# Two token tiles in one product at the small levels of a gated linear attention, in a one-core decoder block

## The chip, the cores and the metric

The kernel runs on one core of one Trainium2 chip. The metric is the device time of one execution in microseconds (us). The kernel before took 900.85 us in the median of three runs (900.52 to 900.86). One execution was recorded by the hardware profiler; it took 900.46 us, of which the profile shows a span of 898.7 us, from the first to the last recorded instruction.

## What is computed

The reference is one layer of a decoder with 512 tokens and width 1024, all in float32: a LayerNorm of the input, a combined input projection, a gated linear attention (GLA) with 4 heads beside a latent attention (MLA) with 8 heads, a gated merge and an output projection, then a squared-ReLU MLP of hidden width 4096, each sub-layer followed by a LayerNorm. The change touches the GLA scores only. Cut to them:

```python
def gla_chunked(q, k, v, log_a):          # per head: 512 tokens, dk 128, dv 256
    # S_t = diag(a_t) S_{t-1} + k_t^T v_t,  o_t = q_t S_t
    b = cumsum(log_a)
    scores[i, j] = sum_d q[i, d] * k[j, d] * exp(b[i, d] - b[j, d])    # j <= i
    o = scores @ v
```

The reference does it in chunks of 64 with a carried state; the kernel computes the scores of all 512 tokens directly.

## The kernel before, in words

**Names.** P is 128 (the partitions), T is 512 (the tokens), NT is 4 (token tiles of 128), GH is 4 heads. Tokens are on the free axis of `qk[:, 0]` (keys) and `qk[:, 1]` (queries), with the 128 channels of a head on the partitions.

**The levels.** The decay of a score is exp(b_i - b_j), a number per channel, so that it has to be put into the two operands of a product without overflow. `gla_levels(h)` (L606) does this by halving. At level s = 1, 2, 4 up to 256 the 512 tokens are cut into blocks of 2s tokens; a score belongs to level s if its key is in the left half of a block and its query in the right half. For these the decay splits into two factors, both at most one, from the running sums in `rp`: one from the key to the border of the halves, one from the border to the query. `vec(s)` makes, for each level, E = exp(rp/16) on ScalarE (L624), then M = E times the left keys and the right queries on VectorE (L626), and `advance(s)` carries the sums in `rp` on to the next level with two additions on GpSimd (L619, L620). So E, the two additions and the next E follow one another.

**The products.** For levels 2 to 64, L680 makes one product per token tile: the stationary operand is the tile's 128 columns of M (keys and queries together; at levels 32 and 64 only the first 96 or 64), the moving operand its 64 right queries. Only the rows of left keys, and of these only those whose block is the query's, hold wanted scores. A float32 product is issued as two passes on TensorE, each with its own load of the stationary operand, so that a level and head have 8 passes. Levels 128 (L684) and 256 (L688) have two products each. Level 1 is made together with the diagonal by L663.

**The selection.** `take(s, p)` copies the wanted scores out of PSUM into `SD` (128 keys by 4 tiles by 128 queries, float32) with a predicated copy on VectorE (L636), under a mask `lmask` per level. The mask comes from DRAM as int32 (`lmi`) and is cast to uint8 once (L415). At a head's end SD is split into a high part (ScalarE, L697) and a remainder (GpSimd, L698) in `sd`, which `gla_out(h)` (L703) uses as stationary operands against the values.

**The order of the work.** The large products (`gemm_fm`, L221; `gemm_tm`, L246) run over steps k of two 128-row slices of weights each. After each step they call `tick`, which advances the side lanes (Python generators) by one `yield`: `lane_levels` goes through the levels of heads 0 to 3, and `lane_out` through the outputs. While `proj_v(0)`, `proj_r(0)`, `proj_v(1)`, `proj_r(1)` and the gate products run, the lanes fill in. `proj_v(1)` has a guard that steps `lane_levels` until head 1 is done, before its results are taken out of PSUM (L904, L912). The instructions of each engine are put into a fixed order by a planner that simulates the program at build time with a cost model, with the order of issue as the priority; on the chip every engine then follows its list, and TensorE waits at a product whose operand isn't there. `tc.issue_after(x)` holds what is issued on x's engine behind x.

**Buffers.** Products of the lanes go into 4 PSUM banks with the tag px; the large ones into 4 others (mm). SBUF tiles come from the pools A (24 slots), B (22 slots) and small ones. Weights come through `pump` (L157): a DMA on the SP queue, then a high part on ScalarE (L180) and a remainder on VectorE (L181), one entry ahead of the product that uses it.

The lines of the level products are these:

```python
for tt in range(NT):
    c = slice(tt * P, (tt + 1) * P)
    mm(p[:rows(s), tt * 64:(tt + 1) * 64].rearrange("p (n s) -> p n s", s=s),
       M[:, tt * P:tt * P + rows(s)], pairs(M[:, c], s)[:, :, 1, :], start=True, stop=True)
```

Of the kernel before, what the change touches and what calls it, by code (L numbers as in the profile page):

```python
# [19 lines left out]
P = 128  # L20
# [32 lines left out]
def tile_hybrid_block(ctx: ExitStack, tc: tile.TileContext, I, out, dbg=None):  # L53
# [22 lines left out]
    def B(shape, dt=F32, n="b"):  # L76
        return pb.tile(shape, dt, tag="B", name=nm(n))
# [10 lines left out]
    def f(ap):  # L88
        return ap.bitcast(F32)
# [256 lines left out]
    def ln_rows(src, dst, mv, on_act=False):  # L346
        bst = S([P, 2, 6], F32, "bst")
        for j in range(2):
            nc.vector.bn_stats(bst[:, j, :], src[:, j * T:(j + 1) * T])
        nc.vector.bn_aggr(mv, bst)  # L350
        vts(mv[:, 1:2], mv[:, 1:2], LN_EPS, None, op0=ALU.add)  # L351
        gtt(mv[:, 1:2], mv[:, 1:2], mhalf[:, 0:1], op=ALU.pow)  # L352
        if on_act:
            nmr = S([P, 1], F32, "nmr")
            stt(nmr, mv[:, 0:1], -1.0, mv[:, 1:2], op0=ALU.mult, op1=ALU.mult)
            act(dst, src, AF.Identity, scale=mv[:, 1:2], bias=nmr)
        else:
            vts(dst, src, mv[:, 0:1], mv[:, 1:2], op0=ALU.subtract, op1=ALU.mult)
# [38 lines left out]
    qag, kvg, glg, bga, bgt, ln1g, ln1b, neg, invf = [cb[:, cut[i]:cut[i + 1]] for i in range(9)]  # L397
    posi = consts.tile([P, NT], I32, name="posi")
    nc.scalar.dma_start(posi, I["positions"].rearrange("(t p) -> p t", p=P))
    lmask = consts.tile([P, len(LEVELS), 64], U8, name="lmask")  # L400
    lmi = B([P, len(LEVELS), 64], I32, "lmi")
    nc.scalar.dma_start(lmi, I["c_lmask"])
    wa2 = B([80, T], F32, "wa2")
    nc.gpsimd.memset(wa2, 0.0)
    for i in range(3):
# [3 lines left out]
    sn2 = consts.tile([P, NT, ROPE], F32, name="sn2")  # L409

    def prep():
        with tc.issue_after(last_in.ins):
            vts(hbg, bgt, 0.5, None, op0=ALU.mult)
            nc.vector.tensor_copy(negb, neg)
            nc.vector.tensor_copy(lmask, lmi)  # L415
        posf = consts.tile([P, NT], F32, name="posf")
        with tc.issue_after(last_in.ins):
            nc.vector.tensor_copy(posf, posi)
        ang = B([P, NT, 32], F32, "ang")
        for tt in range(NT):  # L420
            vts(ang[:, tt, :], invf, posf[:, tt:tt + 1], None, op0=ALU.mult)
        yield
        angs = []
        for sh in (0.0, 0.25):
            kq = B([P, NT, 32], F32, "kq")
            vts(kq, ang, 1.0 / (2.0 * math.pi), sh, op0=ALU.mult, op1=ALU.add)
            vts(kq, kq, MAGIC, None, op0=ALU.add)
            vts(kq, kq, MAGIC, None, op0=ALU.subtract)
            r = B([P, NT, 32], F32, "rr")
            stt(r, kq, -TWO_PI_1, ang, op0=ALU.mult, op1=ALU.add)  # L430
            stt(r, kq, -TWO_PI_2, r, op0=ALU.mult, op1=ALU.add)
            stt(r, kq, -TWO_PI_3, r, op0=ALU.mult, op1=ALU.add)
            vts(r, r, sh * 2.0 * math.pi, PI_F, op0=ALU.add, op1=ALU.min)
            vts(r, r, -PI_F, None, op0=ALU.max)
            angs.append(r)
            yield
        act(sn2[:, :, 32:], angs[0], AF.Sin)
        act(cs2[:, :, :32], angs[1], AF.Sin)
        nc.vector.tensor_copy(cs2[:, :, 32:], cs2[:, :, :32])
        vts(sn2[:, :, :32], sn2[:, :, 32:], -1.0, None, op0=ALU.mult)  # L440
        yield
# [158 lines left out]

    SS = [None] * GH

    def rows(s):
        return P - s if s >= 32 else P

    def gla_levels(h):  # L606
        qk = QK[h]
        QK[h] = None
        rp = A([P, 2, T], F32, "rp")
        nc.vector.tensor_copy(rp[:, 1, :], GL[h])  # L610
        nc.gpsimd.memset(rp[:, 0, :], 0.0)
        SD = B([P, NT, P], F32, "SD")
        SDf = SD.rearrange("p t i -> p (t i)")
        s128 = s256 = None

        def advance(s):
            Rv, Pv = pairs(rp[:, 0, :], s), pairs(rp[:, 1, :], s)
            n = T // (2 * s)
            gtt(Rv[:, :, 0, :], Rv[:, :, 0, :], Pv[:, :, 1, s - 1:s].to_broadcast([P, n, s]), op=ALU.add)  # L619
            gtt(Pv[:, :, 1, :], Pv[:, :, 1, :], Pv[:, :, 0, s - 1:s].to_broadcast([P, n, s]), op=ALU.add)  # L620

        def vec(s):
            E = B([P, T], F32, "E")
            act(pairs(E, s), lr(rp, s), AF.Exp, scale=1.0 / 16.0)  # L624
            M = B([P, T], F32, "M")
            vtt(pairs(M, s), pairs(E, s), lr(qk, s), op=ALU.mult)  # L626
            if s < 256:
                advance(s)
            return M

        def take(s, p):
            nonlocal s128, s256
            if s <= 64:
                n, m = 64 // s, rows(s)
                mk = lmask[:m, LEVELS.index(s), :].rearrange("p (n s) -> p n s", s=s)
                nc.vector.copy_predicated(  # L636
                    SDf[:m].rearrange("p (t n two s) -> p t n two s", t=NT, two=2, s=s)[:, :, :, 1, :],
                    mk[:, None].to_broadcast([m, NT, n, s]),
                    p[:m, :256].rearrange("p (t n s) -> p t n s", t=NT, s=s))
            elif s == 128:  # L640
                s128 = B([P, 2, 2, P], F32R, "s128")
                split(p[:, :256].rearrange("p (a b) -> p a b", b=P), s128[:, 0], s128[:, 1])
            else:
                s256 = A([P, 2, 2, 2 * P], F32R, "s256")
                split(p.rearrange("p (a b) -> p a b", b=256), s256[:, 0], s256[:, 1])


        q1 = B([P, NT, 64], F32, "q1")
        act(q1, pairs(rp[:, 1, :], 1)[:, :, 1, :], AF.Exp, scale=1.0 / 16.0)  # L649
        xs = [B([P, 2, 192], F32, "x1") for _ in range(2)]  # L650
        for i in range(2):
            t2 = slice(2 * i * P, 2 * (i + 1) * P)
            act(xs[i][:, :, :P], qk[:, 1, t2].rearrange("p (t i) -> p t i", i=P), AF.Copy)
            vtt(xs[i][:, :, P:], q1[:, 2 * i:2 * i + 2, :],
                qk[:, 1, t2].rearrange("p (t n two) -> p t n two", t=2, two=2)[:, :, :, 1], op=ALU.mult)
        advance(1)
        yield
        px1 = []
        for i in range(2):
            p = PX()  # L660
            for t in range(2):
                c = slice((2 * i + t) * P, (2 * i + t + 1) * P)
                mm(p[:, t * 192:(t + 1) * 192], qk[:, 0, c], xs[i][:, t, :], start=True, stop=True)  # L663
            px1.append(p)
        s = 2
        M = vec(2)
        yield
        for i, p in enumerate(px1):
            pt = p[:, :384].rearrange("p (t c) -> p t c", c=192)
            d = SD[:, 2 * i:2 * i + 2, :]  # L670
            vtt(d, pt[:, :, :P], ident[:, None, :].to_broadcast([P, 2, P]), op=ALU.mult)
            nc.vector.copy_predicated(d.rearrange("p t (n two) -> p t n two", two=2)[:, :, :, 1],
                                      lmask[:, 0, None, :].to_broadcast([P, 2, 64]), pt[:, :, P:])
        prev = None
        while s < T:
            p = PX()
            if s <= 64:
                for tt in range(NT):
                    c = slice(tt * P, (tt + 1) * P)
                    mm(p[:rows(s), tt * 64:(tt + 1) * 64].rearrange("p (n s) -> p n s", s=s),  # L680
                       M[:, tt * P:tt * P + rows(s)], pairs(M[:, c], s)[:, :, 1, :], start=True, stop=True)
            elif s == 128:
                for i in range(2):
                    mm(p[:, i * P:(i + 1) * P], M[:, 2 * i * P:(2 * i + 1) * P],  # L684
                       M[:, (2 * i + 1) * P:(2 * i + 2) * P], start=True, stop=True)
            else:
                for j in range(2):
                    mm(p[:, j * 256:(j + 1) * 256], M[:, j * P:(j + 1) * P], M[:, 256:], start=True, stop=True)  # L688
            if prev is not None:
                take(*prev)  # L690
            prev = (s, p)
            s *= 2
            if s < T:
                M = vec(s)
            yield
        sd = A([P, 2, NT, P], F32R, "sd")
        act(sd[:, 0], SD, AF.Copy)  # L697
        gtt(sd[:, 1], SD, f(sd[:, 0]), op=ALU.subtract)  # L698
        take(*prev)
        SS[h] = (sd, s128, s256)  # L700
        yield

# [188 lines left out]
    lv = [False] * GH  # L891

    def lane_levels():
        for h in range(GH):
            yield from gla_levels(h)
            lv[h] = True
# [143 lines left out]

    def ln2_stats(tt, j, w=T, c0=0):
        if LN2[tt] is None:
            LN2[tt] = (S([P, 4 if tt == 3 else 2, 6], F32, f"bst{tt}"), S([P, 2], F32, "mv"))
        c = j * T + c0
        i = 2 * j + c0 // w if tt == 3 else j
        nc.vector.bn_stats(LN2[tt][0][:, i, :], res[tt][:, c:c + w])
# [242 lines left out]
```

## Time and profile before

| | |
|---|---|
| median of three runs | 900.85 us |
| the profiled execution | 900.46 us |
| its span | 898.7 us |
| its mean granted TensorE clock | 0.997 of full speed |
| instructions | 11716 |

In the profile, PE is TensorE's matmuls and PEld its loads of the stationary operand, DVE is VectorE, ACT ScalarE, POOL GpSimd and SP the engine that issues the weight DMAs. A line number Lnnn is a line of the kernel file. A row of a group gives the line, the engine, the operation, the tile written, the tiles read, the count and the durations. The table of stretches gives each engine's busy time in a stretch of the span, the granted TensorE clock and the share of the DMA engines. The chain of work that ended last goes back from the last instruction, at each step to what released it; its rows give start and length in us, and an instruction there counts only from the end of the one before it.

### The profile page before, as it was taken

How to read it: one execution, taken by the hardware profiler on the slowest of the kernel's cores; microseconds unless marked ns; L12 is line 12 of the kernel's file. 1: busy time of each engine (PE TensorE's matmuls, PEld its weight loads, DVE VectorE, ACT ScalarE, POOL GpSimd, SP SyncE). 2: the span in 40 equal slices, each digit the busy share in tenths (PEclk: the TensorE clock that was granted, in tenths of full speed). 3: DMA queues.
4: the chain of work that ended last, by engine and by line, in shares of the span. 5: the costliest groups of instructions: out<-in, count | busy, mean ns of one | idle time of the engine just before them, and what ended most of it. 6: DMA issues, size and time to landing. Idle time of an engine off the chain costs nothing.

```text
span 898.7 us, 11716 instructions
## 1 busy us (share of the span) xinstructions
PE 878.0 (98%) x4472; PEld 746.2 (83%) x4472; DVE 570.2 (63%) x927; ACT 432.7 (48%) x731; POOL 172.8 (19%) x201
## 2 busy tenths in 40 slices
PE   5999999999999999999999999999999999999995
PEld 5988888888888888888888888988888888888884
DVE  7835855575634243657765797998556656753687
ACT  5555443444444333435644424266457536644661
POOL 0003542443511010000000002103400520142022
PEclk9999999999999999999999999999999999999998
DMA  7413223212213332212206628004960991298075
GB/s 237 129 47 94 73 69 94 71 47 71 71 42 94 88 107 55 87 35 72 94 24 257 190 69 287 18 1 102 317 144 0 268 251 44 59 307 196 1 187 94
DMA packets 63048, 100.94 MB, mean 112 GB/s; under 512 B 7649, under 2 KB 31585, under 8 KB 62993
## 3 DMA queue, kind: packets, MB, share of 16 engines
q1 hardware_dynamic: 48256, 64.04, 23.2%
q0 software_dynamic: 12816, 32.51, 14.9%
q10 hardware_dynamic: 1920, 3.66, 1.2%
q8 instruction: 35, 0.57, 0.3%
q14 instruction: 21, 0.16, 0.1%
HBM read 82.36 MB, written 3.67 MB: 96 GB/s over the span
## 4 chain that ended last, share of the span: by engine, by line
PE 96%; ACT 1%; DVE 1%; POOL 1%; DMA 1%; issue 0%; POOLq 0%; SPq 0%; DVEq 0%; ACTq 0%
PE mm L231 16%; PE mm L233 15%; PE mm L232 15%; PE mm L264 6%; PE mm L266 6%; PE mm L265 6%; PE px L1134 3%; PE px L1135 3%; PE px L1136 3%; PE mm L1134 2%; PE mm L1135 2%; PE mm L1136 2%; PE px L680 2%; PE px L837 1%; PE px L266 1%; PE px L264 1%
## 5 line engine op out<-in xcount | busy, mean ns | idle before, releaser
L181 DVE TENSOR_TENSOR wlo<-wraw,whi 128x1024 fp32r<-128x1024 f32 (+1 forms) x104 | 117.7, 1133 | 164.4 <-ACT whi L180 157.1
L231 PE MATMUL mm<-h,whi 128*128 128x512 f32 x416 | 162.7, 392 | 0.4 <-ACT gt L924 0.4
L232 PE MATMUL mm<-h,whi 128*128 128x512 f32 x416 | 162.4, 390 | 0.0
L180 ACT ACTIVATE whi<-wraw 128x1024 fp32r<-128x1024 f32 (+1 forms) x104 | 100.3, 964 | 120.6 <-PE mm L232 69.8
L233 PE MATMUL mm<-h,wlo 128*128 128x512 f32 x416 | 154.9, 390 | 0.0
L1162 POOL DMA_DIRECT2D res<-ev x54 | 46.8, 978 | 240.1 <-ACT ev L1160 192.0
L231 PEld LDWEIGHTS mm<-h,whi 128*128 128x128 f32 x416 | 78.1, 188 | 16.4 <-ACT gt L924 0.6
L233 PEld LDWEIGHTS mm<-h,wlo 128*128 128x128 f32 x416 | 77.9, 188 | 16.3 <-DVE wlo L181 0.3
L232 PEld LDWEIGHTS mm<-h,whi 128*128 128x128 f32 x416 | 78.2, 188 | 15.6
L265 PE MATMUL mm<-wlo,h 128*128 128x512 f32 x128 | 50.3, 393 | 0.0
L266 PE MATMUL mm<-whi,h 128*128 128x512 f32 x128 | 50.2, 392 | 0.0
L264 PE MATMUL mm<-whi,h 128*128 128x512 f32 x128 | 49.7, 403 | 0.0
L1216 ACT ACTIVATE relu<-mm 128x512 f32<-128x512 f32 x32 | 18.8, 595 | 56.8 <-PE mm L233 56.8
L352 POOL TENSOR_TENSOR mv<-mv,mhalf 128x1 f32<-128x1 f32 x4 | 4.6, 1155 | 211.9 <-DVE mv L351 211.9
L619 POOL TENSOR_TENSOR rp<-rp 128x256 f32<-128x256 f32 x32 | 31.6, 986 | 60.3 <-ACT E L624 43.6
L626 DVE TENSOR_TENSOR M<-E,qk 128x512 f32<-128x512 f32 x32 | 26.9, 840 | 16.6 <-ACT E L624 16.6
L624 ACT ACTIVATE E<-rp 128x512 f32<-128x512 f32 x32 | 20.4, 638 | 27.7 <-POOL rp L620 27.7
L181 DVE TENSOR_TENSOR wlo<-wq,whi 128x1024 fp32r<-128x1024 f32 x15 | 18.3, 1223 | 19.7 <-ACT whi L180 19.7
L180 ACT ACTIVATE xh<-wraw 128x1024 fp32r<-128x1024 f32 (+1 forms) x20 | 18.7, 953 | 24.8 <-PE mm L266 15.8
L620 POOL TENSOR_TENSOR rp<-rp 128x256 f32<-128x256 f32 x32 | 28.5, 891 | 10.3 <-ACT q L649 8.1
L266 PEld LDWEIGHTS mm<-whi,h 128*128 128x128 f32 x128 | 24.1, 188 | 5.0
L265 PEld LDWEIGHTS mm<-wlo,h 128*128 128x128 f32 x128 | 24.1, 188 | 4.3
(374 smaller groups left out, 2237.7 us busy)
## 6 DMA issues: line engine op xcount, KB each, us to landing
wraw<-in_w_in_dram SPq DMA_DIRECT2D x40, 512.0 KB, 3.6
wraw<-in_w_ff_dram SPq DMA_DIRECT2D x32, 512.0 KB, 8.1
wq<-in_w_ff_dram POOLq DMA_DIRECT2D x32, 512.0 KB, 8.8
res<-ev POOLq DMA_DIRECT2D x54, 256.0 KB, 8.6
wraw<-in_w_o_gla_dram SPq DMA_DIRECT2D x8, 512.0 KB, 3.7
wraw<-in_w_o_mla_dram SPq DMA_DIRECT2D x8, 512.0 KB, 3.4
wraw<-in_w_out_dram SPq DMA_DIRECT2D x8, 512.0 KB, 4.4
wraw<-in_w_in_dram SPq DMA_DIRECT2D x8, 360.0 KB, 5.1
```

What stands on the lines that cost most here:

```text
L180: st["ins"] = act(hi[:, :nk, :n], raw[:, :nk, :n], AF.Copy)
L181: vtt(lo[:, :nk, :n], raw[:, :nk, :n], f(hi[:, :nk, :n]), op=ALU.subtract)
L231: mm(o, hi[:, c], xh, start=first, stop=False)
L232: mm(o, hi[:, c], xl, start=False, stop=False)
L233: mm(o, lo[:, c], xh, start=False, stop=last)
L264: mm(o, xh, hi[:, :n], start=opens, stop=False, skip_group_check=share)
L265: mm(o, xh, lo[:, :n], start=False, stop=False, skip_group_check=share)
L266: mm(o, xl, hi[:, :n], start=False, stop=last, skip_group_check=share)
L1134: mm(o, xh[:, c], hi[:, pp, cols], start=opens, stop=False, skip_group_check=True)
L1135: mm(o, xh[:, c], lo[:, pp, cols], start=False, stop=False, skip_group_check=True)
L1136: mm(o, xl[:, c], hi[:, pp, cols], start=False, stop=hf == 1 and pp == 1, skip_group_check=True)
L1162: nc.gpsimd.dma_start(res[tt + t][:, j * T:(j + 1) * T], e, accum_op=ALU.add)
```

## The change

At levels 2 to 64 two token tiles go into one product. The first half of the tokens is tiles 0 and 1, the second half tiles 2 and 3. `packed` writes M so that tile u of the first half and tile 2 + u share two 128-column operands: in M[:, 0, u] stand the left keys of tile u beside the right queries of tile 2 + u, in M[:, 1, u] the right queries of tile u beside the left keys of tile 2 + u. One product of the two then holds the scores of tile u as before (key by query) and those of tile 2 + u transposed (query by key); the cross terms are not wanted. So there are two products per level and head, with 128 moving columns, in place of four with 64. M is written by two VectorE operations of 256 elements per partition in place of one of 512.

The mask gets an axis for the two halves, and one for u: its second half is the same mask read from DRAM again, shifted by s rows (seven small DMAs on GpSimd's queue after a memset), and the cast to uint8 becomes two casts at the start of `lane_levels`. Level 1 uses the keys as the moving operand for tiles 2 and 3 instead of the queries. At a head's end the tiles 2 and 3 of SD are transposed back by two transposes on TensorE into a px bank, and after one more `yield` they are split from there by ScalarE and VectorE; tiles 0 and 1 are split as before, at half the size. `lmi` moves from pool B to pool A, and the small statistics tile of the last LayerNorm from a pool of its own to pool B.

```diff
-        gtt(mv[:, 1:2], mv[:, 1:2], mhalf[:, 0:1], op=ALU.pow)
+        st["pow"] = gtt(mv[:, 1:2], mv[:, 1:2], mhalf[:, 0:1], op=ALU.pow)
...
-    lmask = consts.tile([P, len(LEVELS), 64], U8, name="lmask")
-    lmi = B([P, len(LEVELS), 64], I32, "lmi")
-    nc.scalar.dma_start(lmi, I["c_lmask"])
+    lmask = consts.tile([P, len(LEVELS), 2, 2, 64], U8, name="lmask")
+    lmi = A([P, 2, len(LEVELS), 64], I32, "lmi")
+    nc.scalar.dma_start(lmi[:, 0], I["c_lmask"])
...
     def prep():
+        with tc.issue_after(st["pow"].ins):
+            nc.gpsimd.memset(lmi[:, 1], 0)
+        for li, s in enumerate(LEVELS):
+            nc.gpsimd.dma_start(lmi[s:, 1, li], I["c_lmask"][:P - s, li])
...
-            nc.vector.tensor_copy(lmask, lmi)
...
+        def packed(M, s, i):
+            v = M[:, i, 0, :]
+            return bass.AP(tensor=v.tensor, offset=v.offset,
+                           ap=[v.ap[0], [2 * s, P // s], [s + (-2 * P if i else 2 * P), 2], [1, s]])
...
-            M = B([P, T], F32, "M")
-            vtt(pairs(M, s), pairs(E, s), lr(qk, s), op=ALU.mult)
+            if s > 64:
+                M = B([P, T], F32, "M")
+                vtt(pairs(M, s), pairs(E, s), lr(qk, s), op=ALU.mult)
+            else:
+                M = B([P, 2, 2, P], F32, "M")
+                for i in range(2):
+                    vtt(packed(M, s, i), pairs(E[:, 2 * i * P:2 * (i + 1) * P], s), half_lr(qk, s, i), op=ALU.mult)
...
-                n, m = 64 // s, rows(s)
-                mk = lmask[:m, LEVELS.index(s), :].rearrange("p (n s) -> p n s", s=s)
-                nc.vector.copy_predicated(
-                    SDf[:m].rearrange("p (t n two s) -> p t n two s", t=NT, two=2, s=s)[:, :, :, 1, :],
-                    mk[:, None].to_broadcast([m, NT, n, s]),
-                    p[:m, :256].rearrange("p (t n s) -> p t n s", t=NT, s=s))
+                mk = lmask[:, LEVELS.index(s)].rearrange("p o u (n s) -> p o (u n) s", s=s)
+                nc.vector.copy_predicated(taken(SD[:, 0, :], s, 2 * P - s), mk, taken(p[:, :2 * P], s, -s))
...
-                for tt in range(NT):
-                    c = slice(tt * P, (tt + 1) * P)
-                    mm(p[:rows(s), tt * 64:(tt + 1) * 64].rearrange("p (n s) -> p n s", s=s),
-                       M[:, tt * P:tt * P + rows(s)], pairs(M[:, c], s)[:, :, 1, :], start=True, stop=True)
+                for u in range(2):
+                    mm(p[:, u * P:(u + 1) * P], M[:, 0, u, :], M[:, 1, u, :], start=True, stop=True)
...
-        act(sd[:, 0], SD, AF.Copy)
-        gtt(sd[:, 1], SD, f(sd[:, 0]), op=ALU.subtract)
+        p = PX()
+        for u in range(2):
+            nc.tensor.transpose(p[:, u * P:(u + 1) * P], SD[:, 2 + u, :], ident)
+        act(sd[:, 0, :2], SD[:, :2], AF.Copy)
+        gtt(sd[:, 1, :2], SD[:, :2], f(sd[:, 0, :2]), op=ALU.subtract)
         take(*prev)
+        yield
+        pt = p[:, :2 * P].rearrange("p (u i) -> p u i", i=P)
+        split(pt, sd[:, 0, 2:], sd[:, 1, 2:])
...
     def lane_levels():
+        for o in range(2):
+            nc.vector.tensor_copy(lmask[:, :, o], lmi[:, o, :, None, :].to_broadcast([P, len(LEVELS), 2, 64]))
...
-            LN2[tt] = (S([P, 4 if tt == 3 else 2, 6], F32, f"bst{tt}"), S([P, 2], F32, "mv"))
+            LN2[tt] = (B([P, 4 if tt == 3 else 2, 6], F32, "bst"), S([P, 2], F32, "mv"))
```

More of the change, by code (lines that the diff above doesn't have):

```diff
@@ L601, in tile_hybrid_block @@
     SS = [None] * GH
-    def rows(s):
-        return P - s if s >= 32 else P
     def gla_levels(h):
@@ L612, in gla_levels @@
         SD = B([P, NT, P], F32, "SD")
-        SDf = SD.rearrange("p t i -> p (t i)")
         s128 = s256 = None
@@ L620, in advance, with half_lr, taken @@
             gtt(Pv[:, :, 1, :], Pv[:, :, 1, :], Pv[:, :, 0, s - 1:s].to_broadcast([P, n, s]), op=ALU.add)
+        def half_lr(t2, s, i):
+            v = t2[:, 0, :]
+            return bass.AP(tensor=v.tensor, offset=v.offset + 2 * i * P,
+                           ap=[v.ap[0], [2 * s, P // s], [T + s, 2], [1, s]])
+        def packed(M, s, i):
+            v = M[:, i, 0, :]
+            return bass.AP(tensor=v.tensor, offset=v.offset,
+                           ap=[v.ap[0], [2 * s, P // s], [s + (-2 * P if i else 2 * P), 2], [1, s]])
+        def taken(v, s, step):
+            return bass.AP(tensor=v.tensor, offset=v.offset + s, ap=[v.ap[0], [step, 2], [2 * s, P // s], [1, s]])
         def vec(s):
@@ L651, in gla_levels @@
         for i in range(2):
-            t2 = slice(2 * i * P, 2 * (i + 1) * P)
-            act(xs[i][:, :, :P], qk[:, 1, t2].rearrange("p (t i) -> p t i", i=P), AF.Copy)
+            side = qk[:, 1 - i, 2 * i * P:2 * (i + 1) * P]
+            act(xs[i][:, :, :P], side.rearrange("p (t i) -> p t i", i=P), AF.Copy)
             vtt(xs[i][:, :, P:], q1[:, 2 * i:2 * i + 2, :],
-                qk[:, 1, t2].rearrange("p (t n two) -> p t n two", t=2, two=2)[:, :, :, 1], op=ALU.mult)
+                side.rearrange("p (t n two) -> p t n two", t=2, two=2)[:, :, :, 1 - i], op=ALU.mult)
         advance(1)
@@ L662, in gla_levels @@
                 c = slice((2 * i + t) * P, (2 * i + t + 1) * P)
-                mm(p[:, t * 192:(t + 1) * 192], qk[:, 0, c], xs[i][:, t, :], start=True, stop=True)
+                mm(p[:, t * 192:(t + 1) * 192], qk[:, i, c], xs[i][:, t, :], start=True, stop=True)
             px1.append(p)
@@ L671, in gla_levels @@
             vtt(d, pt[:, :, :P], ident[:, None, :].to_broadcast([P, 2, P]), op=ALU.mult)
-            nc.vector.copy_predicated(d.rearrange("p t (n two) -> p t n two", two=2)[:, :, :, 1],
-                                      lmask[:, 0, None, :].to_broadcast([P, 2, 64]), pt[:, :, P:])
+            nc.vector.copy_predicated(d.rearrange("p t (n two) -> p t n two", two=2)[:, :, :, 1 - i],
+                                      lmask[:, 0, i], pt[:, :, P:])
         prev = None
```

## The prediction, as it was made

> **What bounds the kernel now.** I read the page first: the busy times, then the chain of work that ended last.
>
> ```profile
> span 898.7 us, 11716 instructions
> PE 878.0 (98%) x4472; PEld 746.2 (83%) x4472; DVE 570.2 (63%) x927; ACT 432.7 (48%) x731; POOL 172.8 (19%) x201
> PE 96%; ACT 1%; DVE 1%; POOL 1%; DMA 1%; issue 0%; POOLq 0%; SPq 0%; DVEq 0%; ACTq 0%
> ```
>
> Two readings agree on TensorE (PE): 98% of the span is busy, 96% of the chain is its own instructions. The next view, who waited for whom on PE, says how much of it is waiting:
>
> ```profile
> PE px L367 <- ACT x L356: 9.1, 1, 9.1
> PE mm L233 <- DVE wlo L181: 0.5, 1, 0.5
> PE mm L231 <- ACT gt L924: 0.4, 1, 0.4
> ```
>
> One wait of 9.1 us is that for the first rows of x; after it no wait exceeds 0.5 us. So PE time taken away anywhere later shortens the span by as much, unless a new wait appears. The levels lie between 104 and 260 us, and the table of stretches shows what is there:
>
> ```profile
> 100.00:140.00 40.00, 40.00 (x219) 34.22 (x218) 27.64 (x47) 18.25 (x33) 20.36 (x24) 1.00 0.24 68
> 220.00:260.00 40.00, 39.57 (x222) 34.08 (x221) 21.61 (x34) 17.24 (x31) 15.65 (x17) 1.00 0.19 52
> 260.00:300.00 40.00, 40.00 (x221) 34.38 (x220) 15.86 (x32) 16.16 (x30) 4.13 (x5) 1.00 0.32 93
> ```
>
> The columns are length, then PE, PEld, DVE, ACT and POOL busy, the granted clock, the DMA share and GB/s. PE is full, DVE at most 69%, DMA a quarter. In the last stretch the levels are over, and PE is still full of large products at 93 GB/s: weights can arrive faster than the level stretches (52 to 68 GB/s) ask for, so they do not become the limit when these shrink.
>
> **The products: what PE gets back.** The busy time of pipelined matmuls is no price; the chain is, since there an instruction counts only from the end of the one before. How many passes there are stands in the group by tile:
>
> ```profile
> L680 PE MATMUL px<-M x192: 216/273/276, 104.8 to 254.3; 128*128 128x64 f32 x128, 128*96 128x64 f32 x32, 128*64 128x64 f32 x32
> L626 DVE TENSOR_TENSOR M<-E,qk x32: 678/694/1162, 101.0 to 252.5; 128x512 f32<-128x512 f32 x32
> ```
>
> 192 passes are 24 groups (6 levels, 4 heads) of 8: 16 groups with 128 stationary columns (levels 2 to 16), 4 with 96, 4 with 64. The chain prices one of each:
>
> ```profile
> 163.57 0.65 PE px L680 x8
> ...
> 165.71 0.61 PE px L680 x8
> 166.31 0.43 PE mm L264
> ...
> 172.21 0.44 PE px L684 x4
> 172.65 0.23 PE mm L265
> ...
> 175.84 0.86 PE px L688 x4
> ...
> 194.56 0.84 PE px L680 x8
> 195.39 0.29 PE mm L264
> ...
> 202.22 0.45 PE px L743 x4
> ```
>
> A large product costs 0.23 in a row of its like. A group with 128 columns costs 0.84 and makes the product behind it 0.29, 0.06 more than 0.23; other such followers lie nearer to 0.23, so I charge 0.05: 0.89. The 96-column group costs 0.65. The 64-column group costs 0.61, and the product behind it 0.20 more: 0.81. Now the new group: two products, 4 passes, 128 stationary and 128 moving columns. The trace has exactly that shape, L684 at level 128: 0.44, with nothing on its follower.
>
> Before: 16 x 0.89 + 4 x 0.65 + 4 x 0.81 = 20.1 us. After: 24 x 0.44 = 10.6 us. **Gain 9.5 us**; without the followers (16 x 0.84 + 4 x 0.65 + 4 x 0.61 = 18.5) it is 7.9, which I keep as the lower end. Level 1 (L663) keeps its shapes and costs the same.
>
> Why doubling the moving columns is nearly free shows in the same rows: per pass, 64 moving columns take 0.84 / 8 = 0.105, 128 take 0.44 / 4 = 0.11, 256 (L688) take 0.86 / 4 = 0.215. Above 128 the moving columns set the price; below it something of about 0.105 does, and it falls with fewer stationary columns (96: 0.65 / 8 = 0.081), so it is the load of the stationary operand. The Trainium skill has a rule against this change (TensorE: Matmul & The Clock Gate, "What happens when you issue a matmul"): throughput is purely the number of moving columns. By that rule 4 x 64 and 2 x 128 columns cost the same and the gain on products is nothing; that is a rival below. The same page's section on LDWEIGHTS makes the load proportional to the stationary columns, 128 / 1.2 = 107 ns, and by this the sum is the one above; the trace's 0.105 agrees.
>
> **Transposes back.** Two per head, 8 in all. L743 is this operation, a float32 transpose of 128 x 128 by the identity: four in 0.45, 0.11 each, **0.9 us lost**. They read SD, complete after the take of level 64, two steps earlier, so they should not wait.
>
> **VectorE and ScalarE beside it.** At 24 places one multiplication of 512 elements (0.69, L626) becomes two of 256. Nearest rows for those, and for the tail of a head:
>
> ```profile
> L107 DVE TENSOR_TENSOR a<-hr,a x16: 407/417/420, 590.7 to 854.6; 128x256 fp32r<-128x256 f32 x16
> ```
>
> ```profile
> L698 POOL TENSOR_TENSOR sd<-SD,sd x4: 1287/1293/1296, 125.6 to 255.8; 128x512 fp32r<-128x512 f32 x4
> ```
>
> A pair takes 2 x 0.42 = 0.84, 0.15 more, 3.5 us in all, and 0.42 per head for the new split. The output of a pair is written in runs of s elements, which no row shows; I bound a half by 0.35 (half of 0.69) and 0.69 (no saving from half the size) and take 0.42. POOL's remainder halves from 1.29 to about 0.65. ScalarE's copy of SD is cut in two of half size. Some 6 us more on DVE in 155 us, of which about 60% is used, are hidden. Cover of the products: the tightest I found is level 32 of head 3:
>
> ```profile
> 243.52 0.69 DVE L626 TENSOR_TENSOR M<-E,qk 128x512 f32<-128x512 f32 x1 [0.86 <-ACT E L624]
> ```
>
> ```profile
> 246.03 0.81 PE L680 MATMUL px<-M 128*96 128x64 f32 x8
> ```
>
> M is ready at 244.21 and read at 246.03: 1.8 us of cover for 0.15 us (at 0.69 a half, 0.7). If the cover were gone, every 0.1 us would cost 24 x 0.1 = 2.4 us, as PE takes its list in order.
>
> **The mask.** The cast was one of 448 elements; now there are two of 896 at the first step of the lane, near 95 us.
>
> ```profile
> L415 DVE CAST lmask<-lmi x1: 383/383/383, 21.9 to 21.9; 128x448 uint8<-128x448 int32 x1
> ```
>
> ```profile
> 102.91 0.42 DVE L552 TENSOR_TENSOR krl<-kr,krh 128x256 fp32r<-128x256 f32 x1 [1.24 <-ACT krh L551]
> 104.17 1.23 DVE L181 TENSOR_TENSOR wlo<-wraw,whi 128x1024 fp32r<-128x1024 f32 x1 [0.83 <-ACT whi L180]
> ```
>
> In proportion each is 0.77, 1.5 us together (bounds 0.4 and, at L626's rate, 1.2 each). What queues behind them on DVE is head 0's start and one weight remainder; the brackets show DVE idle 1.24 and 0.83 shortly after, 2.1 us that absorb it. Uncovered, it is 1.5 us once. The seven mask DMAs and the memset sit on POOL's queue behind the last LayerNorm power:
>
> ```profile
> 66.91 6.11 POOL L535 TENSOR_TENSOR g<-g,az 128x512 f32<-128x512 f32 x4 [40.81 <-ACT az L532]
> ```
>
> ```profile
> L1077 POOL DMA_DIRECT2D wq<-in_w_ff_dram x32: 720/762/1029, 545.8 to 793.3; - x32
> ```
>
> An issue on POOL is 0.76, seven are 5.3 us plus about 0.5 for the memset; POOL is idle for 40.8 us there, so they cost nothing. Without that cover 5.8 us would delay L535 and the start of the levels. The lmi and bst tiles only change pools; I charge nothing, and up to 0.5 us either way through the plan.
>
> **The extra step.** Each head takes 12 steps of the lane in place of 11. Up to the guard of proj_v(1) there are 8 + 8 + 7 = 23 ticks; head 1 ended exactly at the 23rd, now two steps are forced there, ahead of the evacuation of V. That puts one split of 256 (0.42 on DVE) ahead of the bank release: zero to 1 us. At the far end nothing is pressed:
>
> ```profile
> L743 PE MATMUL px<-ca,og x32: 270/272/281, 176.8 to 278.9; 128*128 128x128 f32 x32
> ```
>
> ```profile
> L933 DVE SCALAR_TENSOR_TENSOR gt<-gt,mm x8: 686/687/689, 352.2 to 397.5; 128x512 f32<-128x512 f32 x8
> ```
>
> The lane's last transposes are at 279; their reader is the product whose first result leaves at 352, after 96 products of 0.23, so it begins near 330. Four steps of some 4 us fit.
>
> **Sum.** 9.5 - 0.9 = 8.6 us less on PE, less 0.5 for new short waits (I bound them by 0 and 2): **8.1 us**. The profiled execution took 900.46, 1.76 more than its span; the median is 900.85, 0.39 above it. 900.85 - 8.1 = **892.7 us**. The ends: 7.9 - 0.9 - 2 = 5.0 gained gives 895.9; 9.1 gained (no new wait, and the 0.5 at L233 gone) gives 891.7.
>
> **Rivals.**
> - *The tail of a head takes part back.* The transposes' px bank is held over a step, while lane_out holds two banks and level 256 another: four of four. If PE waits at each head for a split (0.42 on DVE and about as much on ACT, some 1 us), 4 us go: 896.7. Against it: before, the same four can be held in mid-level (two by lane_out, two by successive levels) and PE never waited for it.
> - *The change doesn't do what it says to time.* If moving columns set the price, only the transposes count: 900.85 + 0.9 = 901.8. The rows of 64, 128 and 256 columns speak against it.
> - *Slower: the chain E to E becomes the pace.* A level's E waits for two POOL additions, and head 3 already ran at that pace:
>
> ```profile
> 240.15 0.64 ACT E L624
> 240.86 0.66 POOL rp L619
> 241.59 1.24 POOL rp L620
> ```
>
> ```profile
> L619 POOL TENSOR_TENSOR rp<-rp x32: 615/866/1698, 95.1 to 250.1; 128x256 f32<-128x256 f32 x32
> ```
>
>  Evacuations on ACT queue behind a waiting E; that was the 0.4 us at L231. A link is now about 0.64 + 0.9 + 0.9 = 2.4 us, against a tick of 12 x 0.23 + 0.44 = 3.2. POOL's addition varies from 0.62 to 1.70 for one shape. If the added DVE operations push both to 1.5, a link is 3.65, 0.45 too long, 28 times: 12.6 lost, 905.4. It turns to slower where a link passes 3.2 + 8.1 / 28 = 3.5. Against it: PE is full now at the same POOL work. GPSIMD Engine Reference of the Trainium skill ("Key points") says POOL shares its SBUF interfaces with DVE where that has two SBUF inputs; no row here tells that apart from other causes of the spread.
>
> **Chances.** Forecast (891.7 to 895.9) 0.77; tail 0.10; no gain on products 0.04; chain 0.06; a replanned order that gains more than 9.1 0.03. The range reaches below to 890.0 for the last and above to 897.5 for the tail, and leaves out the other two. A measurement here can tell about 0.2%, 1.8 us, from no change. Faster: 0.77 + 0.10 + 0.03, less 0.01 for a costlier tail, 0.89; same 0.05; slower 0.06.
>
> **What would show it.** Right: 96 passes with 128 moving columns in place of 192, groups of 4 at 0.44 in the chain, 8 more transposes at 0.11, PE busy about 869 to 870, and no PE wait above 0.5 us after 40 us. Wrong: groups near 0.85 (no gain on products); waits of PE for px banks or for M; L231 or L264 waiting behind E on ACT; L619 and L620 well above 0.9; or gaps after 260 us, where nothing changed but the plan.

## The result, and the profile after

The changed kernel takes **893.84 us** (median of six runs, 893.0 to 894.35); the kernel before took 900.68 beside it (six runs, 900.31 to 901.01). The ratio is 0.9925, with a 95% interval of 0.9914 to 0.9936: 6.8 us less. Forecast were 8.1 us less.

The page's first lines, and who waited for whom on PE (us in total, times, longest):

```profile
span 891.8 us, 11595 instructions
PE 869.8 (98%) x4384; PEld 738.2 (83%) x4384; DVE 579.0 (65%) x956; ACT 432.2 (48%) x735; POOL 170.7 (19%) x209
```

```profile
PE px L367 <- ACT x L356: 9.3, 1, 9.3
PE mm L266 <- DVE h L375: 0.7, 1, 0.7
PE px L367 <- DVE lnt L374: 0.6, 1, 0.6
PE mm L233 <- DVE wlo L181: 0.5, 1, 0.5
PE mm L264 <- ACT h L370: 0.5, 1, 0.5
PE mm L231 <- ACT h L370: 0.3, 1, 0.3
```

PE's busy time fell by 878.0 - 869.8 = 8.2 us, but the span by 6.9 only: PE's idle time rose by 1.3, from 20.7 to 22.0. The waits of L266 and L264 for the transposed rows of x (L370, L375) are new, and they belong to the start; the 0.4 us of L231 behind ScalarE is gone. Outside the span lie 1.8 us in the profiled execution before (900.46 - 898.7) and 2.1 in the one after (893.91 - 891.8). The table of stretches puts the loss in its place (length, then PE, PEld, DVE, ACT, POOL busy); the first fence is the kernel before, the second the one after:

```profile
0.00:40.00 40.00, 30.54 (x181) 29.10 (x182) 31.83 (x75) 23.35 (x39) 4.37 (x9) 1.00 0.66 205
```

```profile
0.00:40.00 40.00, 28.89 (x169) 27.02 (x170) 31.22 (x69) 22.25 (x38) 7.76 (x17) 1.00 0.67 210
...
100.00:140.00 40.00, 40.00 (x204) 34.07 (x203) 31.92 (x64) 19.00 (x36) 19.75 (x28) 1.00 0.27 79
...
220.00:260.00 40.00, 40.00 (x210) 34.23 (x209) 24.89 (x43) 18.04 (x35) 14.70 (x17) 1.00 0.22 63
```

In the level stretches PE stays full, with DVE at up to 80%. In the first 40 us, before any level runs, PE does 30.54 - 28.89 = 1.65 us less. That is what is new or longer in the list of waits: 0.7 at L266, 0.5 at L264, and 0.2 at each of the two waits of L367, which were 9.1 and 0.4 before. So the levels gave about what was forecast, and something in the start took 1.65 us back.

The level products, by tile and then in the chain (start, length counted from the end of the instruction before):

```profile
L692 PE MATMUL px<-M x96: 270/275/275, 106.6 to 246.5; 128*128 128x128 f32 x96
L643 DVE TENSOR_TENSOR M<-E,qk x48: 406/526/956, 102.5 to 242.7; 128x256 f32<-128x256 f32 x48
```

```profile
116.68 0.44 PE px L692 x4
117.13 0.23 PE mm L265
...
122.82 0.44 PE px L692 x4
123.26 0.45 PE px L695 x4
...
178.35 0.23 PE px L710 x2
```

96 passes, 0.44 a group of four, nothing on the product behind it, and 0.23 for two transposes (L710). These are the prices that the prediction took from L684 and L743.

What moved in the start is seen in the load of lmi, on ScalarE's queue, and in SP's queue. First before, then after:

```profile
L402 ACTq DMA_DIRECT2D lmi<-in_c_lmask_dram x1: 352/352/352, 17.2 to 17.2; - x1
```

```profile
2.12 9.53 SPq L168 DMA_DIRECT2D wraw<-in_w_in_dram  x4
11.69 0.47 SPq L121 DMA_DIRECT2D x<-in_x_dram  x1
```

```profile
L912 DVE CAST lmask<-lmi x2: 683/685/687, 13.1 to 36.8; 128x896 uint8<-128x896 int32 x2
L402 ACTq DMA_DIRECT2D lmi<-in_c_lmask_dram x1: 352/352/352, 10.1 to 10.1; - x1
```

```profile
2.12 10.55 SPq L168 DMA_DIRECT2D wraw<-in_w_in_dram  x5
12.72 0.46 SPq L121 DMA_DIRECT2D x<-in_x_dram  x1
```

The load is issued at 10.1 us in place of 17.2; the third tile of x is issued behind five weight loads instead of four, 1 us later; and the two casts, which I had put near 95 us, run on VectorE at 13.1 and 36.8, in the middle of the start. Each of these could be the cause.

### The profile page after: what moved, and what is told of

Same layout as the page of the kernel before. It is cut to its first block, busy times and chain, and to the rows that moved or that the text cites. A ratio compares the mean times of both kernels' runs of the same rounds, so it can differ in the third digit from the quotient of the medians.

```text
span 891.8 us, 11595 instructions
## 1 busy us (share of the span) xinstructions
PE 869.8 (98%) x4384; PEld 738.2 (83%) x4384; DVE 579.0 (65%) x956; ACT 432.2 (48%) x735; POOL 170.7 (19%) x209
## 4 chain that ended last, share of the span: by engine, by line
PE 95%; DMA 2%; DVE 1%; issue 0%; ACT 0%; SPq 0%; POOLq 0%; DVEq 0%; POOL 0%; ACTq 0%
PE mm L231 16%; PE mm L233 16%; PE mm L232 16%; PE mm L264 5%; PE mm L266 5%; PE mm L265 5%; PE px L1153 3%; PE px L1154 3%; PE px L1155 3%; PE mm L1154 2%; PE mm L1155 2%; PE mm L1153 2%; DMA wraw<-in_w_in_dram 1%; PE px L692 1%; PE px L854 1%; PE px L266 1%
## 5 line engine op out<-in xcount | busy, mean ns | idle before, releaser
L231 PE MATMUL mm<-h,whi 128*128 128x512 f32 x416 | 162.8, 393 | 0.0
L233 PE MATMUL mm<-h,wlo 128*128 128x512 f32 x416 | 155.3, 390 | 0.0
L233 PEld LDWEIGHTS mm<-h,wlo 128*128 128x128 f32 x416 | 78.1, 188 | 16.1
L231 PEld LDWEIGHTS mm<-h,whi 128*128 128x128 f32 x416 | 78.2, 188 | 15.8
L266 PE MATMUL mm<-whi,h 128*128 128x512 f32 x128 | 50.2, 394 | 0.0
L264 PE MATMUL mm<-whi,h 128*128 128x512 f32 x128 | 49.9, 400 | 0.0
L618 POOL TENSOR_TENSOR rp<-rp 128x256 f32<-128x256 f32 x32 | 29.9, 935 | 63.5 <-ACT E L636 52.8
L643 DVE TENSOR_TENSOR M<-E,qk 128x256 f32<-128x256 f32 x48 | 28.9, 628 | 12.4 <-ACT E L636 12.1
L266 PEld LDWEIGHTS mm<-whi,h 128*128 128x128 f32 x128 | 24.1, 188 | 4.8
L264 PEld LDWEIGHTS mm<-whi,h 128*128 128x128 f32 x128 | 23.9, 188 | 4.2
```

Source lines behind the costliest of these rows:

```text
L231: mm(o, hi[:, c], xh, start=first, stop=False)
L233: mm(o, lo[:, c], xh, start=False, stop=last)
L264: mm(o, xh, hi[:, :n], start=opens, stop=False, skip_group_check=share)
L266: mm(o, xl, hi[:, :n], start=False, stop=last, skip_group_check=share)
```

## The experiments

**Theory 1, the pool.** `lmi` went from pool B to pool A. The supposition is that in B it has to wait for a slot, so that its load is planned late, and that in A a slot is free at once, the load goes early, and the start is ordered anew around it. **Theory 2, the casts.** Without the gate that the cast had before, two casts of 0.69 us run in the start and delay the rows there. Both explain the new waits; a rival to the accounting itself is that the level products are priced otherwise than by passes.

### lmi in pool B

The memset, the seven mask DMAs and the casts then name the two tiles `lmi[0]` and `lmi[1]`; cut to the pool:

```diff
-    lmi = A([P, 2, len(LEVELS), 64], I32, "lmi")
-    nc.scalar.dma_start(lmi[:, 0], I["c_lmask"])
+    lmi = [B([P, len(LEVELS), 64], I32, "lmi") for _ in range(2)]
+    nc.scalar.dma_start(lmi[0], I["c_lmask"])
...
```

> The changed kernel with lmi as two tiles of pool B instead of one of pool A; all else as it is. Theory 1 (the pool): in A the tile has a free slot at once, its load is planned at 10 us ahead of weights and rows of x, and the start loses 1.6 us of PE; back in B the load goes behind them again, so the time falls by 1.6 us to about 892.2 and PE busy in the first 40 us returns from 28.9 to about 30.5. Theory 2 (the casts): the two casts planned at 13.1 and 36.8 us on VectorE hold the start up; they stay here, so the time stays at 893.8.

Measured: 892.31 us against 900.24 before; ratio 0.9910 (0.9896 to 0.9923). The first stretch, PE's waits, the casts and the load of lmi:

```profile
0.00:40.00 40.00, 30.70 (x181) 29.45 (x182) 31.24 (x71) 22.91 (x39) 8.10 (x17) 1.00 0.66 210
```

```profile
PE px L367 <- ACT x L356: 9.1, 1, 9.1
PE mm L233 <- DVE wlo L181: 0.5, 1, 0.5
PE mm L231 <- ACT h L370: 0.3, 1, 0.3
PE px L367 <- DVE lnt L374: 0.2, 1, 0.2
```

```profile
L912 DVE CAST lmask<-lmi x2: 680/682/684, 22.0 to 48.1; 128x896 uint8<-128x896 int32 x2
L402 ACTq DMA_DIRECT2D lmi<-in_c_lmask_dram x1: 347/347/347, 17.2 to 17.2; - x1
```

The load is back at 17.2, the start's new waits are gone, PE's busy time there is that of before, as theory 1 expected. But the casts did not stay where they were, as the expectation had assumed: they moved from 13.1 and 36.8 to 22.0 and 48.1. This run alone therefore doesn't tell the two theories apart; the next two do.

### Before, with lmi in pool A

```diff
-    lmi = B([P, len(LEVELS), 64], I32, "lmi")
+    lmi = A([P, len(LEVELS), 64], I32, "lmi")
```

> The kernel before with nothing changed but the pool of lmi, A instead of B; the one cast and the level products as before. Theory 1: the start loses 1.6 us, 902.3, PE busy in the first 40 us 28.9 instead of 30.5. Theory 2: no change, 900.7.

Measured: 903.02 against 900.24; ratio 1.0027 (1.0017 to 1.0037), **2.8 us slower from one letter**, where theory 1 had expected 1.6. The same stretch, and the first of the waits:

```profile
0.00:40.00 40.00, 28.92 (x166) 27.26 (x167) 29.82 (x64) 21.72 (x37) 4.20 (x9) 1.00 0.64 205
```

```profile
PE px L367 <- ACT x L356: 9.0, 1, 9.0
PE mm L266 <- DVE h L375: 1.3, 2, 0.8
PE mm L264 <- ACT h L370: 0.8, 1, 0.8
```

The new waits stand here without a single changed level product, with one cast of the old size. Theory 1's cause, the pool, holds; theory 2 expected no change.

### The casts held back

```diff
-        nc.vector.tensor_copy(QK[a][:, 0, :], ps)
+        st["k"] = nc.vector.tensor_copy(QK[a][:, 0, :], ps)
...
-        for o in range(2):
-            nc.vector.tensor_copy(lmask[:, :, o], lmi[:, o, :, None, :].to_broadcast([P, len(LEVELS), 2, 64]))
+        with tc.issue_after(st["k"].ins):
+            for o in range(2):
+                nc.vector.tensor_copy(lmask[:, :, o], lmi[:, o, :, None, :].to_broadcast([P, len(LEVELS), 2, 64]))
```

> The changed kernel with the two mask casts held behind the last copy of the keys on VectorE (near 94 us); lmi stays in pool A. Theory 2: the start is freed of 1.4 us of VectorE, 892.3 to 892.5. Theory 1: no gain at the start, 893.8, or up to 0.5 more if the casts hold up the first level.

Measured: 894.85 against 900.24; ratio 0.9939 (0.9926 to 0.9951). No gain: theory 2 falls. The median is 0.5 above the most that theory 1 had allowed, with five runs that spread from 893.70 to 895.91.

```profile
PE mm L266 <- DVE h L375: 2.1, 2, 1.9
```

The wait at the start is there without the casts, and longer; PE does 28.41 us of work in the first 40, against 28.89 with the casts there. Held back, the casts keep lmi's slot in pool A longer, but before the second cast of the changed kernel, at 36.8, that is no difference.

### Pool A and pool B on one chip

No edit: the changed kernel, and the first experiment's kernel beside it.

> The changed kernel as it is, on the same chip as the next three, so that the pools of lmi can be compared within one chip. 893 to 894; theory 1 wants it 1.6 us above the next run.

> The changed kernel with lmi in pool B, beside the changed kernel on one chip. Theory 1: 1.6 us less than the changed kernel, 892.2. If the gain of the first run of it was the chip's, no difference.

Measured: 894.40 with lmi in A (ratio to before 0.9932, 0.9919 to 0.9946), 892.23 with lmi in B (0.9912, 0.9899 to 0.9926); before 900.25. The pool costs 2.2 us on this chip, and with it put right the change gains 900.25 - 892.23 = 8.0 us. The eleven runs of the changed kernel in the two sets (893.0 to 894.48) all lie above the eight with lmi in B (891.62 to 892.98). The version with lmi in B beats both kernels.

### Moving columns or the load

```diff
-                    mm(p[:rows(s), tt * 64:(tt + 1) * 64].rearrange("p (n s) -> p n s", s=s),
-                       M[:, tt * P:tt * P + rows(s)], pairs(M[:, c], s)[:, :, 1, :], start=True, stop=True)
+                    mm(p[:rows(s), c], M[:, tt * P:tt * P + rows(s)], M[:, c], start=True, stop=True)
```

The selection then takes the right halves out of p.

> The kernel before with all 128 columns of a tile as the moving operand at levels 2 to 64 (64 of them unused), still four products per level and head; the result is the same. If the load of the stationary operand sets the price of a pass, a group of 8 passes costs 8 x 0.11 = 0.88 at any stationary width of 128 or less: 16 x (0.88 - 0.89) + 4 x (0.88 - 0.65) + 4 x (0.88 - 0.81) = +1.0 us, 901.7. If the moving columns set it, 64 more cost 64 x (0.86 - 0.44) / (4 x 128) = 0.053 a pass, 192 passes 10.1 us: 910.8.

Measured: 902.53 against 900.24; ratio 1.0024 (1.0015 to 1.0033), 2.3 us more. The chain:

```profile
104.90 0.89 PE px L680 x8
105.79 0.23 PE mm L264
...
119.49 0.87 PE px L680 x8
...
208.86 1.02 PE px L680 x8
209.88 0.43 PE mm L264
```

With 128 stationary columns, twice the moving columns cost 0.89 in place of 0.84 + 0.05: nothing. The rule of pure moving columns (10.1 us more) is out. With 96 stationary columns the group goes to 0.87, as expected of 128 moving ones. Not expected: with 64 stationary columns it is 1.02, and the product behind it still pays 0.20. By these rows a run of all levels costs 16 x 0.89 + 4 x 0.87 + 4 x 1.22 = 22.6, 2.5 more than 20.1; measured 2.3, where the load alone would have given 1.0. That it is the load that sets the price below 128 moving columns is argued and not shown: at levels 32 and 64 the number of stationary columns and the length of the runs of s tokens change together. The gain of the change doesn't hang on it.

### The level products twice

```diff
-                for u in range(2):
+                for u in (0, 1, 0, 1):
                     mm(p[:, u * P:(u + 1) * P], M[:, 0, u, :], M[:, 1, u, :], start=True, stop=True)
```

> lmi in pool B with the products of levels 2 to 64 made twice into the same bank: 24 groups become 8 passes. At 0.11 a pass 24 x 0.44 = 10.6 us more, 902.8. If moving columns beyond the load were free or the group price were mostly a fixed start, 3 to 6 us more.

Measured: 902.25 against 899.92 before; ratio 1.0024 (1.0014 to 1.0033). Against lmi in pool B that is 10.0 us by the medians (892.2) and 10.2 by the ratios (0.9911), since the two ran on different chips; forecast were 10.6. In the chain:

```profile
116.55 0.89 PE px L692 x8
```

So 24 groups of four passes are worth about 10 us, measured in time, not only in the chain.

### The tail of a head: four runs

All four have lmi in pool B. The first leaves out the transposes back and the step added for them:

```diff
-        p = PX()
-        for u in range(2):
-            nc.tensor.transpose(p[:, u * P:(u + 1) * P], SD[:, 2 + u, :], ident)
-        act(sd[:, 0, :2], SD[:, :2], AF.Copy)
-        gtt(sd[:, 1, :2], SD[:, :2], f(sd[:, 0, :2]), op=ALU.subtract)
+        act(sd[:, 0], SD, AF.Copy)
+        gtt(sd[:, 1], SD, f(sd[:, 0]), op=ALU.subtract)
         take(*prev)
-        yield
-        pt = p[:, :2 * P].rearrange("p (u i) -> p u i", i=P)
-        split(pt, sd[:, 0, 2:], sd[:, 1, 2:])
```

The second takes only the line `yield` away, so that the transposes stay and the added step goes. The third is the first with `yield` kept: the step without the transposes. The fourth makes the transposes twice, with `for u in (0, 1, 0, 1)`.

> lmi in pool B, and the transposes back left out with the step added for them: SD is split whole as in the kernel before, so that the scores of tiles 2 and 3 stay transposed and the output is not the reference's. Term of the sum: 8 transposes at 0.11 are 0.9 us; 0.9 less than lmi in pool B, 891.3. If head ends cost PE waits (the rival on the tail), 2 to 4 us less.

> lmi in pool B, and the split of the transposed tiles in the same step as the transposes: the added step is gone, the result is the same. If the step and the two forced steps at the guard cost nothing, no difference to lmi in pool B (within 0.5 us); if they hold the evacuation of V up, up to 1 us less.

> lmi in pool B with the added step kept and only the transposes back and their split left out: SD is split whole, tiles 2 and 3 stay transposed, the output is not the reference's. If the waits seen without the step (L231 behind ACT 0.5, and with the transposes gone too L734 behind ACT 1.0) come from the missing step, they go and the transposes' 0.9 us show: 891.3. If they come from the changed plan in general, 892 to 893.5 with waits of PE of 0.5 to 2 us.

> lmi in pool B with the two transposes of each head made twice into the same bank: 8 more at 0.11, 0.9 us more than lmi in pool B, 893.1; PE busy 0.9 more. A plan that shifts may add 0.5 to 1.5.

Measured: 893.54 (0.9924, 0.9911 to 0.9936) without either; 893.18 (0.9920, 0.9907 to 0.9934) without the step; 892.23 (0.9910, 0.9896 to 0.9923) without the transposes; 892.44 (0.9913, 0.9900 to 0.9927) with them twice. lmi in pool B stood at 0.9910 and 0.9912. The first missed its forecast by 2.2 us: less work, more time. The second took 0.9 more where none or up to 1 less was expected, and the fourth 0.1 to 0.3 more, by the ratios, where 0.9 was. PE's waits in the first run after those of the start, those without the step, and those with the step and no transposes:

```profile
PE px L734 <- ACT osq L738: 1.0, 1, 1.0
...
PE mm L231 <- ACT gt L937: 0.5, 1, 0.5
...
PE px L692 <- DVE SD L652: 0.4, 1, 0.4
```

```profile
PE mm L231 <- ACT gt L942: 0.5, 1, 0.5
```

```profile
PE px L676 <- DVE x L667: 1.0, 1, 1.0
```

Each plan without the tail's full work brings 0.5 to 1.9 us of waits at other places; after the start the kernel with lmi in B has only the waits of L233 (0.5) and of L231 for L370 (0.3), which all these kernels have. Without the transposes PE's busy time is 868.8 against 869.7 and 870.2 in the two runs of lmi in B, 0.9 to 1.4 less, as the price says, but one wait of 1.0 takes it back. Doubling them adds 0.3 to 0.8 us of busy time (870.5), and its 0.1 to 0.3 us in time lie within the intervals, which span over 2 us. So the transposes cost PE about what was forecast, and in the time of this kernel that cannot be told from zero. No cost of the added step shows: without it the median is higher by 0.9, though the intervals overlap.

## Why the prediction was right, point by point

- **What bounds it.** Right: PE time removed is span removed. 8.2 us less busy, and full PE in all level stretches.
- **The products, 9.5 us.** Right, and shown: groups at 0.44 without a follower's price, twice the groups is 10.0 us more, and 128 moving columns are free beside 128 stationary ones. The change with lmi in B gains 8.0 us where 9.5 - 0.9 - 0.5 = 8.1 was the sum. So close a match is in part luck. The product behind a group with 96 columns pays too, 0.29 behind the one at 119.55 in the kernel before, which the sum left out, 0.2 us at most in all; the 0.5 for new short waits found no counterpart on PE once lmi is in B, and L231's 0.4 went; and the time outside the span grew by 0.3. Such tenths are less than the spread of one kernel's runs, about 1 us, and can't be told apart in time.
- **Transposes, 0.9.** Right in the chain (0.23 for two); in time not resolved.
- **VectorE.** The halves of M were mis-sized: 0.42 was forecast for one, 0.63 is the mean.

```profile
L626 DVE TENSOR_TENSOR M<-E,qk 128x512 f32<-128x512 f32 x32 | 26.9, 840 | 16.6 <-ACT E L624 16.6
```

```profile
L643 DVE TENSOR_TENSOR M<-E,qk 128x256 f32<-128x256 f32 x48 | 28.9, 628 | 12.4 <-ACT E L636 12.1
```

  The first line is the kernel before. By the means a pair takes 1.26 against 0.84 for the one operation, 0.4 more and not 0.15; the 0.69 that the forecast started from is L626's median. VectorE's busy time rose by 8.8 us where some 6 were forecast. The cover of 1.8 us held: PE waits for M nowhere.
- **The mask.** The place was wrong. I put the casts where the program issues them, near 95 us; the planner ran them at 13.1 and 36.8, since nothing held them. Held back to the forecast place in the third experiment, they brought no gain, so no cost of this shows. The duration was 0.69 each, forecast 0.77; the seven DMAs hid on POOL as forecast.
- **The pool of lmi.** This is the step that failed: "The lmi and bst tiles only change pools; I charge nothing, and up to 0.5 us either way through the plan." It cost 1.65 us of PE in the first 40 us of the profile, 2.2 us in time between pools on one chip, and 2.8 us put alone into the kernel before. That is more than the whole difference of 1.3 us between 8.1 and 6.8. The time still came out at 893.8, as the range of 891.7 to 895.9 had room for a term that the sum had put at nothing.
- **The added step.** The guard's two forced steps show no wait; removing the step did not help.
- **The rivals.** No wait for a px bank at the heads' ends. No price by moving columns. The chain from E to E did not slow: POOL's first addition is 0.94 against 0.99 before, whose line stands first.

```profile
L619 POOL TENSOR_TENSOR rp<-rp 128x256 f32<-128x256 f32 x32 | 31.6, 986 | 60.3 <-ACT E L624 43.6
```

```profile
L618 POOL TENSOR_TENSOR rp<-rp 128x256 f32<-128x256 f32 x32 | 29.9, 935 | 63.5 <-ACT E L636 52.8
```

What stays open is how the early load of lmi slows the start. The chain of the changed kernel shows a path (start, length):

```profile
12.30 0.37 SPq L168
...
12.72 4.77 DMA x<-in_x_dram
...
25.39 4.70 DMA wraw<-in_w_in_dram
...
30.11 1.06 ACT whi L180
...
31.53 0.46 ACT h L370
...
32.03 0.43 PE mm L264
```

The fifth weight load goes out at 12.30, after a split on VectorE has ended, and the third tile of x behind it, to land at 17.5. VectorE's next rows wait for that tile and its splits come behind them, the next weights land at 30.1, and the h for which L264 waits is made on ScalarE behind their split. The other three profiles with lmi in pool A have this path too, each with five weight loads ahead of the third tile of x. In the kernel before, and in both profiles with lmi in pool B and no other edit, there are four, and the chain is on PE from 13.5 us on. So the new order in SP's queue is the likely way, but it is not shown: no run moved that load alone, and the run without the step takes nearly this path with four loads ahead and no wait of L264 or L266.

The halves of M take 0.41 to 0.96 us for one shape. The two beside which no addition of GpSimd runs take 0.41, and all 23 of over 0.6 have one beside them for at least 0.4 us. But most of those of about 0.42 have one too, and no run took the additions away, so the cause is open.

## What to carry to other kernels

When PE is the bound, price a product group from the chain, where it counts from the end of its predecessor, together with what the product behind it pays, and look for a row of exactly the new shape; here the sum for the products then came within about a microsecond of what time and busy time show, on 9.5. In a kernel whose order a planner makes, a tile that only changes its pool is not free, here about 2 us of 900: ask when its load can now start, and what moves on the queues there. In the three runs here that took some of the tail's work or its step away, the new plan brought waits of 0.5 to 1.9 us, so gains of about a microsecond have to be measured and not added up.

## What the runs showed of the hardware that was not expected

A float32 pass with only 64 stationary columns (level 64 alone has them) is not the cheapest, once the product behind it is counted. With 64 moving columns eight of them take 0.61 us (0.076 a pass), but with 128 moving columns 1.02 (0.128), more than with 96 (0.87) or 128 (0.89) stationary ones; and in both cases the large product behind pays 0.43 in place of 0.23. A narrow stationary operand thus saved less than its 0.61 showed: 0.81 with its follower, against 0.44 for the whole new group.
